# The recurrence of a two-layer trunk, issued in phases among the dense products: four steps a slot, its small TensorE products without priority

## The chip, the cores and the metric

One NeuronCore of a Trainium2 chip runs the whole program in one launch. The metric is the device time of one execution in microseconds (us). The engines are PE (TensorE, matrix products; PEld is its weight load), DVE (VectorE), ACT (ScalarE), POOL (GpSimd) and SP (which issues the DMAs). Each engine works through its own queue in order, and a semaphore holds an instruction back until what it reads is there.

## The reference, cut to what matters

The model has two layers. Each is SwiGLU, mixer, SwiGLU, with residual adds and a norm ahead of each. The mixer of layer 0 is RWKV-7, that of layer 1 is mLSTM. 512 prompt rows and 32 sample rows (8 sequences of 4) go through it, 544 columns in all.

```python
def rwkv7_time_mix(xn, shift0, S0, ...):
    xr, xw, xk, xv, xa, xg = [xf + xx * mu[c] for c in range(6)]
    r, k, v = xr @ wr, xk @ wk, xv @ wv
    w = -softplus(-(w0 + tanh(xw @ w1) @ w2)) - 0.5
    a = sigmoid(a0 + (xa @ a1) @ a2);  g = sigmoid(xg @ g1) @ g2
    def step(S, inp):
        sa = einsum('bhvk,bhk->bhv', S, -kk_t)
        S = S * d_t + sa[..., None] * b_t + v_t[..., None] * k_t
        return S, einsum('bhvk,bhk->bhv', S, r_t)
    y = groupnorm(scan(step, S0, ...)) + bonus
    return (y * g) @ wo
```

## The kernel before, in words

**Dense products.** Activations lie transposed, 128 features by columns. Columns are cut into two parts: part 0 has 256, part 1 has 288 (256 prompt columns and the 32 of the sample). A weight block comes by DMA into `wr`; ACT casts it to a high half `wh`, DVE subtracts to get the low half `wl` (lines 352 and 353), 512 columns at a time, four buffers of each. `mm3` (lines 355 to 358) then makes three fp32r products of each 128 by 128 block into a PSUM bank `pd`, of which there are two.

**The recurrence.** It works on head pairs. A group `m` is two pairs in one part: groups 0 to 3 are part 0, groups 4 to 7 are part 1. For each group `rwkv_prep` makes decays and keys (tiles `swa`, `a`), `rwkv_quad` squares up a 64 by 64 triangular inverse for its chunks (tiles `b`, `ti`, `p1s`, `tf`), `rwkv_tokens` lays out the values (`uv`), and then four chunks of 64 columns follow each other in `rwkv_chunk`: products into `pr`, `pu`, `pn` (one bank, `pc`), with DVE and ACT copies between, and a new state `sm`. `rwkv_finish` (norm, gate; lines 1151 to 1169) closes a group, `rwkv_sample` does the 32 sample rows of part 1. All their products are small: 64 to 128 rows, 64 to 128 columns mostly, in f32 or f16.

**Slots.** One chunk is a slot, `t` from 0 to 31; slots 0 to 15 are part 0. `rwkv_slots` writes the recurrence of a slot first and then some units of dense work: the rest of the first SwiGLU of part 1 and the first projections of part 1 in slots 0 to 9, its other projections in 10 to 15, nothing in 16, and the output projection of part 0 (`rwkv_out`) with the second SwiGLU of part 0 in 17 to 31. Before the projections of part 1 stands its norm (a product `pd<-rms`), and ahead of each kind of projection a mix: eight times `m` (line 693), a cast, and `mx` (line 695, on DVE and POOL in turn).

**What sets the order.** A list scheduler places every instruction on its engine as soon as it counts it as ready, by priority, and the priority is the place in the program. Inside `high_priority(OFF)`, with OFF = 20000, it counts as 20000 places earlier. The whole recurrence stands inside such a block, so that each of its instructions goes ahead of the dense work as soon as the scheduler has it ready.

Of the kernel before, what the change touches and what calls it, by code (L numbers as in the profile page):

```python
# [17 lines left out]
P = 128  # L18
D = 1024
KT = 8  # L20
# [8 lines left out]
OFF = 20000  # L29
NMX = 19  # L30
# [218 lines left out]

class Trunk:  # L250
    def __init__(self, tc, nc, a, o, pool):
        self.tc, self.nc, self.a, self.o, self.pool = tc, nc, a, o, pool
        self.n = 0
        self.last = None
        self.hn = {}
        self.V, self.S, self.G, self.T = nc.vector, nc.scalar, nc.gpsimd, nc.tensor

# [97 lines left out]
    def mm3(self, out, wh, wl, xh, xl, start, stop):  # L355
        self.T.matmul(out, wh, xh, start=start, stop=False)  # L356
        self.T.matmul(out, wh, xl, start=False, stop=False)  # L357
        self.T.matmul(out, wl, xh, start=False, stop=stop)  # L358
# [102 lines left out]
    def ffn_units(self, name, g, i, groups=(0, 8, 15, FT)):  # L461
# [18 lines left out]
        def up(m):  # L480
            pg, pu = self.bank("pd", 2), self.bank("pd", 2)
            for ps, n in ((pg, "_g"), (pu, "_u")):
                wt = self.weight(self.a[name + n][m])
                for k in range(KT):
                    c = slice(k * P, (k + 1) * P)
                    self.mm3(ps[:, :w_], *wt(c), xs[k][0], xs[k][1], k == 0, k == KT - 1)
            s, w, e = self.t1(w_), self.t1(w_), self.t1(w_)
            V.tensor_tensor(s, pg[:, :w_], rs, op=ALU.mult)  # L488
            V.tensor_tensor(w, pu[:, :w_], rs, op=ALU.mult)
            self.sigmoid(e, s)  # L490
            G.tensor_tensor(s, s, w, op=ALU.mult)
            G.tensor_tensor(s, s, e, op=ALU.mult)
            h[m] = [self.hm(w_) for _ in range(2)]
            self.split(*h[m], s)
# [9 lines left out]
        for k0, k1 in zip(groups, groups[1:]):  # L504
            us += [lambda m=m: up(m) for m in range(k0, k1)]
            us += [lambda m=m, k0=k0, k1=k1: down(m, k0, k1) for m in range(KT)]
# [50 lines left out]
    def rwkv(self, before=None, after=None):  # L557


        with self.scope("rw", nps=1):  # L560
# [4 lines left out]
            with self.tc.tile_pool(name="spill", bufs=1, space=DRAM) as dp:  # L565
# [3 lines left out]
                self.d, self.quad, self.st = {}, {}, {}  # L569
                self.chain, self.chain_y = [self.bank("pc", 2) for _ in range(2)]  # L570
                self.nhm = {"mx": NMX, "hm": 8}
                with self.scope("rw1", nps=0):
# [7 lines left out]
                    with self.tc.high_priority(OFF):  # L580
                        self.rwkv_ahead(0)
                        self.rwkv_square(0)
# [3 lines left out]
                    with self.tc.high_priority(OFF):  # L586
                        self.rwkv_value(0)
                        self.rwkv_ahead(1)
# [6 lines left out]
                with self.scope("rw2", nps=0):  # L595
                    with self.tc.high_priority(OFF):
                        self.rwkv_value(ND)
# [106 lines left out]
    def rwkv_project(self, n, c, i):  # L704
# [12 lines left out]
        return [lambda: xs.extend(self.rwkv_mix(c, i))] + [lambda m=m: unit(m) for m in range(KT)]  # L717

    def rwkv_low_rank(self, i):
# [36 lines left out]
        for c, ns in ((1, (("r_w1", P, slice(0, 64), self.hwa),)), (4, (("r_a1", P, slice(64, P), self.hwa),)),  # L756
                      (5, (("r_g1a", P, slice(0, P), self.hg), ("r_g1b", P, slice(0, 96), None)))):
            us.append(lambda c=c: mix(c))
# [3 lines left out]
    def rwkv_first(self, i):  # L762

        low, k = self.rwkv_low_rank(i), self.rwkv_project("k", 2, i)
        return ([lambda: self.rwkv_norm(i)] + low[:4] + self.rwkv_project("r", 0, i) + k[:5],
# [26 lines left out]
    def rwkv_ahead(self, m):  # L792

        if m < 2 * ND:
            self.d[m] = [self.rwkv_prep(2 * (m % ND) + a, m // ND) for a in range(2)]

    def rwkv_square(self, m):
        if m < 2 * ND:
            self.quad[m] = self.rwkv_quad(self.d[m])

    def rwkv_value(self, m):
        if m < 2 * ND:
            uv = self.rp("uv", 2, [P, 1024]).rearrange("p (a c h v) -> p a c h v", a=2, c=4, h=2)
            for a in range(2):
                self.rwkv_tokens(2 * (m % ND) + a, m // ND, self.d[m][a]["v"], uv[:, a])
            self.quad[m] += (uv,)

    def rwkv_slots(self, t0, t1):

        for t in range(t0, t1):  # L810
            m, c = divmod(t, 4)
            i, j = divmod(m, ND)
            with self.tc.high_priority(OFF):
                if c == 0:
                    self.rwkv_square(m + 1)

                    if m + 1 != ND:
                        self.rwkv_value(m + 1)
                if c == 2:
                    self.rwkv_ahead(m + 2)  # L820
                if i and c in (0, 1):
                    self.rwkv_sample(2 * j + c, self.d[m][c])
# [27 lines left out]
    def rwkv_prep(self, j, i):  # L850
        nc, V, S, G, T = self.nc, self.V, self.S, self.G, self.T
# [10 lines left out]
        for e, rows in enumerate(R):  # L862
            ps = self.bank("pq", 1)[:, :w]
# [12 lines left out]
        S.activation(q, k, AF.Square, scale=self.vec("kk", j))  # L876
        ps = self.bank("pq", 1)[:, :w]
# [29 lines left out]
        return {"xc": xc, "xs": xs, "arc": arc, "ars": ars, "pc": pc, "y": k, "v": v}  # L907

    def rwkv_quad(self, ds):
# [3 lines left out]
        V, S, G, T = self.V, self.S, self.G, self.T  # L913
# [16 lines left out]
        xt = self.rp("xt", 2, [P, 1024])  # L930
        mask = self.maskg.unsqueeze(1).to_broadcast([P, 4, P])
        for a, d in enumerate(ds):
            xc, arc = d["xc"], d["arc"]
            pg = pb()
# [6 lines left out]

        for a, d in enumerate(ds):
            px = self.bank("pq", 1)
            for i in range(4):
                T.transpose(px[:, i * P:(i + 1) * P], flat(d["xc"][:, i]), self.ident)
            S.copy(xt[:, a * 512:(a + 1) * 512], px)
# [10 lines left out]
        e = part(0)  # L957
        pt = pb()
# [5 lines left out]
        for l in range(1, 6):  # L964
            e = part(l)
            p1 = pb()
            each(lambda r, a, b: T.matmul(p1[r, a], e[r, a], ti[r, a], start=True, stop=True))
            p1s = h16("p1s")
            S.copy(p1s, p1[:, :W])
            pd = pb()  # L970
# [7 lines left out]
        pt = pb()  # L978
        each(lambda r, a, b: T.matmul(pt[r, a], ti[r, a], id16[r], start=True, stop=True))
        S.copy(tt, pt[:, :W])  # L980
        pr = pb()

# [615 lines left out]
```

## Time and profile before

| | us |
|---|---|
| median of 3 runs (lowest, highest) | 2540.12 (2539.03, 2542.99) |
| the profiled execution | 2541.78 |
| its span, first to last instruction | 2539.80 |
| PE busy, weight loads busy | 2445.1, 2310.1 |
| DVE, ACT, POOL busy | 1587.1, 1250.3, 501.6 |
| mean granted TensorE clock | 0.976 |

The chunks of the recurrence run from 423 us to 1100 us of the span, its last products at 1212 us. Before and behind it are dense products alone, and the mLSTM stage from about 1840 us. A matmul's row has a duration that is longer than the pitch at which such products follow each other, since they are pipelined; for the cost of a product the distance from start to start is read. The granted clock has two levels, 2.4 GHz (1.00) and 1.2 GHz.

### The profile page before, as it was taken

The numbers are of one execution on the slowest core, as the hardware profiler recorded it, in microseconds if no ns is written. First come the engines' busy times: TensorE is split into PE (matmuls) and PEld (weight loads), VectorE is DVE, ScalarE is ACT, GpSimd is POOL, SyncE is SP. The second block draws the span as 40 slices with busy tenths as digits, with TensorE's granted clock in tenths as the row PEclk, the third lists the DMA queues.
The fourth block names the chain that finished last, engine by engine and source line by source line (L and its number), as shares of the span: only waits on it lengthen the run. The fifth ranks groups of instructions, "written<-read, shape, count | busy, mean of one in ns | idle before, by whom it ended". The sixth has DMA issues, their size and how long they took to land.

```text
span 2539.8 us, 54086 instructions
## 1 busy us (share of the span) xinstructions
PE 2445.1 (96%) x21731; PEld 2310.1 (91%) x21731; DVE 1587.1 (62%) x3154; ACT 1250.3 (49%) x2716; POOL 501.6 (20%) x522
## 2 busy tenths in 40 slices
PE   9998999999889999999999999999999999999997
PEld 8998988888778788897899999999978899999997
DVE  6667787787887886765666544443346856444433
ACT  6555666655575564554555433332245545333322
POOL 1203333333432342322011011110000000111100
PEclk9998999999799899999999999999999999999999
DMA  6664543333233223444455522222223322222222
GB/s 215 183 197 130 166 131 120 105 96 120 90 120 103 75 93 113 129 150 146 128 167 164 153 89 90 84 85 88 83 87 112 101 73 92 86 92 90 88 84 73
DMA packets 102218, 291.62 MB, mean 115 GB/s; under 512 B 12568, under 2 KB 28344, under 8 KB 101968
## 3 DMA queue, kind: packets, MB, share of 16 engines
q1 hardware_dynamic: 101968, 288.18, 36.9%
q8 instruction: 170, 2.79, 0.4%
q14 instruction: 80, 0.66, 0.1%
HBM read 278.76 MB, written 9.38 MB: 113 GB/s over the span
## 4 chain that ended last, share of the span: by engine, by line
PE 84%; DVE 9%; issue 2%; ACT 2%; DMA 1%; POOL 1%; SPq 0%; DVEq 0%; ACTq 0%; POOLq 0%
PE ps L356 17%; PE ps L358 17%; PE ps L357 17%; PE pd L356 7%; PE pd L357 7%; PE pd L358 7%; DVE wl L353 2%; DVE m L693 1%; PE ps L1254 1%; PE ps L1256 1%; PE ps L1255 1%; PE b L937 1%; PE ps L1135 1%; DVE mx L695 1%; PE pc L1059 1%
## 5 line engine op out<-in xcount | busy, mean ns | idle before, releaser
L353 DVE TENSOR_TENSOR wl<-wr,wh 128x512 fp32r<-128x512 f32 (+2 forms) x1025 | 723.2, 708 | 479.6 <-ACT wh L352 452.8
L352 ACT CAST wh<-wr 128x512 fp32r<-128x512 f32 (+2 forms) x1025 | 621.8, 609 | 676.6 <-PE ps L357 430.8
L356 PE MATMUL ps<-a,wh 128*128 128x288 f32 (+1 forms) x2384 | 698.0, 293 | 13.5 <-ACT a L404 5.0
L358 PE MATMUL ps<-a,wl 128*128 128x288 f32 (+1 forms) x2384 | 692.6, 291 | 0.0
L357 PE MATMUL ps<-a,wh 128*128 128x288 f32 (+1 forms) x2384 | 686.6, 288 | 0.3
L356 PEld LDWEIGHTS ps<-a,wh 128*128 128x128 f32 x2384 | 452.8, 190 | 16.9 <-DVE raw L1350 5.4
L357 PEld LDWEIGHTS ps<-a,wh 128*128 128x128 f32 x2384 | 452.6, 190 | 1.5 <-DVE a L405 0.8
L358 PEld LDWEIGHTS ps<-a,wl 128*128 128x128 f32 x2384 | 450.0, 189 | 0.5 <-DVE wl L353 0.2
L428 POOL TENSOR_TENSOR t<-t,t 128x256 f32<-128x256 f32 (+1 forms) x132 | 141.7, 1073 | 846.7 <-ACT wh L352 410.1
L356 PE MATMUL ps<-h,wh 128*128 128x288 f32 (+1 forms) x1056 | 303.9, 288 | 0.0
L357 PE MATMUL ps<-h,wh 128*128 128x288 f32 (+1 forms) x1056 | 303.4, 287 | 0.0
L358 PE MATMUL ps<-h,wl 128*128 128x288 f32 (+1 forms) x1056 | 303.2, 287 | 0.0
L356 PE MATMUL pd<-rk,wh 128*128 128x288 f32 (+1 forms) x656 | 199.0, 304 | 6.8 <-DVE t L488 2.9
L358 PEld LDWEIGHTS ps<-h,wl 128*128 128x128 f32 x1056 | 198.9, 188 | 0.0
L357 PEld LDWEIGHTS ps<-h,wh 128*128 128x128 f32 x1056 | 198.9, 188 | 0.0
L357 PE MATMUL pd<-rk,wh 128*128 128x288 f32 (+1 forms) x656 | 198.6, 303 | 0.2 <-DVE gm L679 0.2
L356 PEld LDWEIGHTS ps<-h,wh 128*128 128x128 f32 x1056 | 198.6, 188 | 0.0
L358 PE MATMUL pd<-rk,wl 128*128 128x288 f32 (+1 forms) x656 | 197.2, 301 | 0.0
L352 ACT CAST h<-t 128x256 fp32r<-128x256 f32 (+1 forms) x132 | 55.3, 419 | 198.9 <-POOL t L428 198.9
L357 PE MATMUL pd<-mx,wh 128*128 128x256 f32 (+1 forms) x448 | 135.3, 303 | 9.4 <-DVE mx L695 6.6
L356 PE MATMUL pd<-mx,wh 128*128 128x256 f32 (+1 forms) x448 | 133.8, 302 | 4.3 <-ACT rk L716 1.9
L356 PEld LDWEIGHTS pd<-rk,wh 128*128 128x128 f32 x656 | 128.0, 195 | 10.5 <-ACT mx L694 2.9
(460 smaller groups left out, 4548.4 us busy)
## 6 DMA issues: line engine op xcount, KB each, us to landing
wr<-in_f0a_u_dram SPq DMA_DIRECT2D x44, 512.0 KB, 3.6
wr<-in_f0b_g_dram SPq DMA_DIRECT2D x44, 512.0 KB, 3.6
wr<-in_f0b_u_dram SPq DMA_DIRECT2D x44, 512.0 KB, 3.5
wr<-in_f0a_g_dram SPq DMA_DIRECT2D x43, 512.0 KB, 3.6
wr<-in_f0b_d_dram SPq DMA_DIRECT2D x24, 512.0 KB, 3.6
wr<-in_f1a_g_dram SPq DMA_DIRECT2D x22, 512.0 KB, 4.6
wr<-in_f1a_u_dram SPq DMA_DIRECT2D x22, 512.0 KB, 3.5
wr<-in_f1b_g_dram SPq DMA_DIRECT2D x22, 512.0 KB, 3.5
```

The lines of the kernel that those rows point to most:

```text
L352: self.S.copy(dst_h, src)
L353: self.V.tensor_tensor(dst_l, src, dst_h, op=ALU.subtract)
L356: self.T.matmul(out, wh, xh, start=start, stop=False)
L357: self.T.matmul(out, wh, xl, start=False, stop=False)
L358: self.T.matmul(out, wl, xh, start=False, stop=stop)
L428: self.G.tensor_tensor(s, s, w, op=ALU.mult)
L693: V.scalar_tensor_tensor(m, d, self.vec("mu", c * 8 + k), xn, op0=ALU.mult, op1=ALU.add)
L695: (self.G if k % 2 else V).tensor_tensor(l, m, h.bitcast(F32), op=ALU.subtract)
L937: T.matmul(pg[:, (1 - h) * 512 + i * P:(1 - h) * 512 + (i + 1) * P], flat(xc[R[h], i]), flat(arc[R[h], i]), start=True, stop=True)
L1059: T.matmul(py[R[h], out(a)], uv[:, a, c, h, :], gm[:, a, c, 1 - h, 64:128], start=True, stop=st is None)
L1135: T.matmul(pn[R[h], :], xt[H, h * 64:(h + 1) * 64], um, start=True, stop=True)
L1254: T.matmul(pss[q][:n, :], xs[k][0][:, ts], wt(cs)[0], start=k == 0, stop=False)
```

## The change

The functions of the recurrence become generators that yield before each group of products that waits for other engines, and name the PSUM bank it needs: "s" (none that is contended), "pq" or "ps". `rwkv_slots` starts the generators and, four times a slot, advances every one by a step at the "s" places, writes some dense work, advances those at "pq" and "ps", and writes dense work again. Dense work is now spread by its number of products (a SwiGLU unit in two halves, a mix counted as none). The products of the recurrence go through `Plain`, which takes the priority of 20000 back: they stand at their place in the program. The instructions of DVE, ACT and POOL keep it. The finish of a group is begun at the end of its last slot and advanced during the next, where it stood at once before.

```diff
+class Plain:
+    def matmul(self, *a, **k):
+        with self.t.tc.high_priority(LEAD - self.t.off):
+            return self.engine.matmul(*a, **k)
...
+    def rwkv_phase(self, places):
+        with self.tc.high_priority(OFF):
+            self.off = OFF
+            seen = set()
+            for name in list(self.gens):
+                place = self.gens[name][1]
+                if place in places and (place == "s" or place not in seen):
+                    seen.add(place)
+                    self.advance(name)
+            self.off = 0
...
     def rwkv_slots(self, t0, t1):
+        total, left, n = sum(c for c, _ in todo), 0, 2 * SPS * (t1 - t0)
+        def dense():
+            k += 1
+            while todo and done + todo[0][0] / 2 <= total * k / n:
+                c, f = todo.pop(0)
+                done += c
+                f()
         for t in range(t0, t1):
...
-                self.rwkv_chunk(m, c)
+                self.begin("chunk", self.rwkv_chunk(m, c))
+            for q in range(SPS):
+                self.rwkv_phase(("s",))
+                dense()
+                self.rwkv_phase(("pq", "ps"))
+                dense()
+                self.drain("chunk")
                 if c == 3:
-                    for a in range(2):
-                        self.rwkv_finish(2 * j + a, i, m)
-            self.step(-(-len(self.todo) // (t1 - t)))
+                    self.drain("finish", "sample")
+                    self.begin("finish", self.rwkv_finishes(m))
+                if t == 4 * ND or t == 8 * ND - 1:
+                    self.drain("finish")
```

SPS is 4, LEAD is 0. Smaller edits: the transposed rows `xt` are made apart from the quad; the quad's last transpose shares a bank with the residual; the sample's first products share banks, and two of its transposes one bank; in a chunk the products `py` stand ahead of the DVE instructions that make the new state.

Three places in the order of the built programs. The first is PE just around the norm of part 1. `uv_9791` is the values tile of group 3, `uv_7641` that of group 2. Before:

```order
L1042 MATMUL pc_2715<-sm_11215,tf_9789 64x64 x4
L387 MATMUL pd_8955<-rms_8932,c_c_all_79 128x288
L1059 MATMUL pc_2716<-gm_9376,uv_9791 64x64
L1048 MATMUL pc_2715<-uv_9791,xt_9377 64x64 x4
L1059 MATMUL pc_2716<-gm_9376,uv_9791 64x64 x3
L1035 MATMUL pc_2715<-uv_9791,gm_9376 64x64 x2
```

Now:

```order
L269 MATMUL pc_2715<-sm_9427,tf_9267 64x64 x4
L416 MATMUL pd_8878<-rms_8855,c_c_all_79 128x288
L269 MATMUL b_9476<-a_1622_8573 128x128 x8
L269 MATMUL ps_9706<-rk_930_4479,c_c_rw_2701 128x256
L269 MATMUL pq_9657<-c_c_all_79,x_69 64x64 x5
L269 MATMUL pc_2716<-gm_7640,uv_7641 64x64
```

The products `sm,tf` of 13 slots stand ahead of this norm in the order before, and of 9 now; at the last product of the projections of part 1 it is 16 in both.

The second is PE in that stretch of projections. `pd_9163` and `pd_8996` are banks of two dense units, `b_9716` is a step of the quad of group 3. Now:

```order
L385 MATMUL pd_9163<-mx_9115,wh_9166 128x288
L269 LDWEIGHTS ti_9572
L269 MATMUL b_9716<-p1s_9655,ti_9572 64x64
L269 LDWEIGHTS ti_9572
L269 MATMUL b_9716<-p1s_9655,ti_9572 64x64
L386 MATMUL pd_9163<-mx_9116,wh_9166 128x288
L387 MATMUL pd_9163<-mx_9115,wl_9167 128x288
L385 MATMUL pd_9163<-mx_9121,wh_9166 128x288
L269 LDWEIGHTS ti_9572
L269 MATMUL b_9716<-p1s_9655,ti_9572 64x64
```

The same step of an earlier group before, of which the 16 products follow each other:

```order
L358 MATMUL pd_6903<-rk_536_2749,wl_6945 128x288
L945 MATMUL pq_7840<-c_c_all_79,a_1392_7225 128x128 x4
L971 LDWEIGHTS ti_6235
L971 MATMUL b_6483<-p1s_6481,ti_6235 64x64
L971 LDWEIGHTS ti_6235
L971 MATMUL b_6483<-p1s_6481,ti_6235 64x64
```

The runs of small products that stand between dense ones are, up to the norm of part 1, to the end of its projections and to the end of the recurrence, 88, 36 and 126 before, and 96, 59 and 149 now.

The third is PE in slot 16. `stp` is the state that group 0 left, `pd_12858` and `pd_12895` are units of the output projection, `rk_2217_12033` is the finished output of the first pair of group 3. Before:

```order
L1118 MATMUL ps_12406<-sb_12404,sa_12363 64x64
L1061 MATMUL pc_2716<-a_1947_10340,stp_7438 64x64
L1059 MATMUL pc_2716<-gm_10796,uv_11877 64x64 x2
L1061 MATMUL pc_2716<-a_1957_10392,stp_7438 64x64 x2
L356 MATMUL pd_12858<-rk_1696_9082,wh_12861 128x256
L357 MATMUL pd_12858<-rk_1697_9083,wh_12861 128x256
L358 MATMUL pd_12858<-rk_1696_9082,wl_12862 128x256
```

Now:

```order
L269 MATMUL pc_2716<-a_1953_10283,stp_7499 64x64 x2
L269 MATMUL pq_12079<-rk_1812_9474,c_c_rw_2701 128x288
L269 MATMUL ps_12027<-a_519_2731,a_520_2732 128x256 x3
L269 MATMUL ps_12027<-a_520_2732 128x256
L269 MATMUL pc_2715<-uv_11822,gm_10743 64x64 x2
L269 MATMUL pc_2715<-sm_12024,a_1930_10119 64x64 x2
L269 MATMUL pc_2715<-uv_11822,gm_10743 64x64 x2
L269 MATMUL pc_2715<-sm_12024,a_1953_10283 64x64 x2
L269 MATMUL ps_12071<-sb_12010,sa_11909 64x64
L385 MATMUL pd_12159<-rk_2217_12033,wh_12166 128x256
L385 MATMUL pd_12225<-rk_2217_12033,wh_12232 128x256
L269 MATMUL pc_2715<-sm_12156,tf_11763 64x64 x4
```

Before, 18 dense products of one bank follow the chunk's; the finish of group 3 stands far ahead of them. Now the finish of group 3 (`ps_12027` is the gate of its first pair) stands in this slot, the first two units of the output projection hold both banks `pd` with all but their last products done, and from there to the last of these, after the finish of the second pair, 12 dense products stand among the small ones.

## Rows read from the trace of the kernel before

**Rows 1.** The page's first part: busy us, share of the span, instructions.
```profile
PE 2445.1 (96%) x21731; PEld 2310.1 (91%) x21731; DVE 1587.1 (62%) x3154; ACT 1250.3 (49%) x2716; POOL 501.6 (20%) x522
```
**Rows 2.** Busy time of each engine in stretches of the span; the first line names the columns.
```profile
core 0: us, PE busy (x) PEld busy (x) DVE busy (x) ACT busy (x) POOL busy (x), PEclk, DMA share, GB/s
420.00:640.00 220.00, 214.87 (x2758) 192.60 (x2756) 174.20 (x359) 134.07 (x312) 71.38 (x67) 0.99 0.36 109
640.00:806.00 166.00, 143.39 (x1221) 128.14 (x1222) 139.75 (x277) 105.87 (x263) 57.28 (x75) 0.87 0.30 93
806.00:1195.00 389.00, 379.02 (x4396) 329.41 (x4397) 275.72 (x585) 211.06 (x492) 126.49 (x129) 0.97 0.39 121
1215.00:1840.00 625.00, 624.29 (x4858) 623.44 (x4858) 319.75 (x579) 260.41 (x493) 71.12 (x66) 1.00 0.38 115
```
**Rows 3.** The same view, for line 357, one of three products of each dense block.
```profile
420.00:640.00 220.00, 99.44 (x331) 62.92 (x330) 0.99 0.36 109
```
**Rows 4.** PE in order of time, 1191 us: start, duration, engine, line, shapes.
```profile
1191.33 0.29 PE L357 MATMUL pd<-rk,wh 128*128 128x288 f32 x1
1191.46 0.29 PE L358 MATMUL pd<-rk,wl 128*128 128x288 f32 x1
1191.59 0.29 PE L356 MATMUL pd<-rk,wh 128*128 128x288 f32 x1
1191.72 0.29 PE L357 MATMUL pd<-rk,wh 128*128 128x288 f32 x1
1191.94 0.33 PE L1118 MATMUL ps<-sb,sa 64*64 64x64 f32 x2
1192.20 0.40 PE L358 MATMUL pd<-rk,wl 128*128 128x288 f32 x1
1192.43 0.29 PE L356 MATMUL pd<-rk,wh 128*128 128x288 f32 x1
```
**Rows 5.** DVE groups of 420 to 640 us: busy us, mean ns, idle before.
```profile
L353 DVE TENSOR_TENSOR wl<-wr,wh 128x512 fp32r<-128x512 f32 (+1 forms) x85 | 62.4, 738 | 17.7 <-ACT wh L352 15.7 <-ACT uv L1011 1.1
L502 DVE SCALAR_TENSOR_TENSOR x<-pd,x 128x288 f32<-128x288 f32 x32 | 14.3, 453 | 3.0 <-PE pd L358 2.8
L353 DVE TENSOR_TENSOR hm<-t,hm 128x288 fp32r<-128x288 f32 x11 | 5.9, 535 | 2.2 <-ACT hm L352 2.1
L489 DVE TENSOR_TENSOR t<-pd,rms 128x288 f32<-128x288 f32 x10 | 4.6, 457 | 4.2 <-PE pd L358 4.0
L488 DVE TENSOR_TENSOR t<-pd,rms 128x288 f32<-128x288 f32 x10 | 4.5, 455 | 2.3 <-PE pd L358 1.4 <-POOL t L491 0.7
L870 DVE TENSOR_TENSOR_SCAN swa<-c_c_scan,swa 128x256 f32<-128x256 f32 x5 | 3.7, 735 | 0.1
L1039 DVE COPY sm<-pc 128x128 f32<-128x128 f32 x12 | 3.4, 284 | 2.8 <-PE pc L1037 1.5 <-PE pc L1035 1.3
L374 DVE TENSOR_TENSOR rms<-rms,t 128x288 f32<-128x288 f32 x6 | 2.7, 452 | 0.0
```
**Rows 6.** The same of 640 to 806 us.
```profile
L693 DVE SCALAR_TENSOR_TENSOR m<-hm,c_vecs,x 128x288 f32<-128x288 f32 x48 | 31.1, 671 | 1.6 <-POOL mx L695 0.6 <-POOL hm L674 0.4
L695 DVE TENSOR_TENSOR mx<-m,mx 128x288 fp32r<-128x288 f32 x24 | 14.4, 601 | 0.8 <-ACT mx L694 0.5
L870 DVE TENSOR_TENSOR_SCAN swa<-c_c_scan,swa 128x288 f32<-128x288 f32 x4 | 3.6, 902 | 0.0
```
**Rows 7.** Busy time again, for the 60 us in which DVE is fullest.
```profile
720.00:780.00 60.00, 48.55 (x377) 42.96 (x376) 56.17 (x114) 40.53 (x97) 24.41 (x23) 0.89 0.28 88
```
**Rows 8.** PE in order of time at the last two finishes, 1200 to 1215 us.
```profile
1200.59 0.82 PE L1151 MATMUL ps<-rk,c_c_rw 128*128 128x288 f32 x2 [0.78 <-DVE s L1136]
...
1207.26 1.33 PE L1151 MATMUL ps<-rk,c_c_rw 128*128 128x288 f32 x2 [1.80 <-DVE rk L1169]
...
1214.72 0.81 PE L356 MATMUL pd<-rk,wh 128*128 128x288 f32 x2 [2.34 <-ACT rk L352]
```

More of the change, by code (lines that the diff above doesn't have):

```diff
@@ L480, in up, with half, second @@
         def up(m):
[L481 to L494, printed above, removed]
+            ps = []
+            def half(n):
+                ps.append(self.bank("pd", 2)[:, :w_])
+                self.part_dense(self.weight(self.a[name + n][m]), ps[-1], xs)
+            def second():
+                half("_u")
+                s, w, e = self.t1(w_), self.t1(w_), self.t1(w_)
+                V.tensor_tensor(s, ps[0], rs, op=ALU.mult)
+                V.tensor_tensor(w, ps[1], rs, op=ALU.mult)
+                self.sigmoid(e, s)
+                G.tensor_tensor(s, s, w, op=ALU.mult)
+                G.tensor_tensor(s, s, e, op=ALU.mult)
+                h[m] = [self.hm(w_) for _ in range(2)]
+                self.split(*h[m], s)
+            return Unit((24, lambda: half("_g")), (24, second))
         def down(m, k0, k1):
@@ L568, in rwkv @@
                 self.v = [[t[:, hs] for t in self.x] for hs in PARTS]
-                self.d, self.quad, self.st = {}, {}, {}
+                self.d, self.quad, self.st, self.xt, self.uv = [{} for _ in range(5)]
                 self.chain, self.chain_y = [self.bank("pc", 2) for _ in range(2)]
@@ L716, in unit @@
             self.S.copy(t, ps)
-        return [lambda: xs.extend(self.rwkv_mix(c, i))] + [lambda m=m: unit(m) for m in range(KT)]
+        return [Unit((0, lambda: xs.extend(self.rwkv_mix(c, i))))] + [lambda m=m: unit(m) for m in range(KT)]
     def rwkv_low_rank(self, i):
@@ L794, in rwkv_ahead @@
         if m < 2 * ND:
-            self.d[m] = [self.rwkv_prep(2 * (m % ND) + a, m // ND) for a in range(2)]
+            self.d[m] = []
+            for a in range(2):
+                yield from self.rwkv_prep(2 * (m % ND) + a, m // ND, self.d[m])
     def rwkv_square(self, m):
         if m < 2 * ND:
-            self.quad[m] = self.rwkv_quad(self.d[m])
+            yield from self.rwkv_quad(m, self.d[m])
     def rwkv_value(self, m):
@@ L993, in rwkv_quad, with rwkv_rows @@
         V.tensor_tensor(tf, tt, pf[:, :W], op=ALU.add)
-        return gm, tf, xt
+        self.quad[m] = gm, tf, self.xt[m]
+    def rwkv_rows(self, m):
+        self.xt[m] = xt = self.rp("xt", 2, [P, 1024])
+        for a, d in enumerate(self.d[m]):
+            yield "pq"
+            px = self.bank("pq", 1)
+            for i in range(4):
+                self.PT.transpose(px[:, i * P:(i + 1) * P], d["xc"][:, i].rearrange("p x t -> p (x t)"), self.ident)
+            self.S.copy(xt[:, a * 512:(a + 1) * 512], px)
     def wide_bank(self):
@@ L1061, in rwkv_chunk @@
                 T.matmul(py[R[h], out(a)], st[R[h], col(a)], arc[a][R[h], c, 1, :], start=False, stop=True)
+        sn = self.rp("stp", ND, [P, P]) if m < ND and c == 3 else self.rp("sm", 3, [P, P])
+        for a in range(2):
+            if st is None:
+                V.tensor_scalar(sn[:, col(a)], pn[:, col(a)], pc[a], None, op0=ALU.mult)
+            else:
+                V.scalar_tensor_tensor(sn[:, col(a)], pn[:, col(a)], pc[a], sp[:, col(a)], op0=ALU.mult, op1=ALU.add)
         if c == 3:
```

187 lines of the change are left out of this document (126 added, 61 removed).

## The prediction

> **What bounds the kernel now.** I read the page's first part, then the busy time by stretches, then the DVE groups of two stretches, then single products in order of time. The page says PE 96%, DVE 62% [rows 1], and the reader is to see that PE is the engine to look at, but that such a share is a mean over stretches with different limits. The stretches show it [rows 2]. Behind the recurrence (1215 to 1840 us) PE is busy 624.29 of 625 us at full clock: dense products alone, which the change does not touch. In the recurrence there are three kinds. From 420 us to the norm of part 1 (640 us) PE is busy 214.87 of 220: PE-bound, with DVE at 79%. From there to the end of the projections of part 1 (806 us) PE is busy only 143.39 of 166 at a granted clock of 0.87, and DVE 139.75, 84%: here the mixes load DVE (`m` and `mx` take 31.1 + 14.4 us of it [rows 6]) and PE waits for what DVE makes. From 806 to 1195 us PE is bound again (379.02 of 389), with DVE at 71%.
>
> Two prices are needed. **A slot.** In the first stretch the dense products are 331 for one of the three lines [rows 3]; at the pitch from start to start, 0.13 us [rows 4], 3 x 331 x 0.13 = 129 us. The other 91 us of the 220 are small products and what they wait for. The state copy `sm<-pc` stands there 12 times [rows 5], one a slot, so 7.6 us of PE a slot. Of DVE, 174.20 less the groups of dense work (62.4 + 14.3 + 5.9 + 4.6 + 4.5 + 2.7 = 94.4 [rows 5]) leaves 79.8, or 6.65 us a slot. **An interruption.** Two tiny products between dense ones [rows 4]: undisturbed the third start is 0.26 us after the first (1191.33 to 1191.59), with the interruption it is 0.71 us (1191.72 to 1192.43). That is 0.45 us, of which perhaps 0.1 is the products' own, an estimate from the 64-column shape beside 288 columns in 0.13; so 0.35 us for breaking the dense stream once, whatever stands in the break.
>
> **The change part by part.** It adds and removes almost no work: the order holds the same dense products and, but for some merged banks, the same small ones; I count those edits at nothing, since what they save is a few tiny products a group in a stretch with hundreds. What changes is where the small ones stand, and five terms follow.
>
> First stretch: the order has 13 slots ahead of the norm before and 9 now. It is PE-bound, so PE time leaves it: 4 x 7.6 = 30 us at most; by the count of small products that leave, about a quarter of what stood there, it is nearer 25. I take 28, range 21 to 31. The order has 8 more interruptions there, 8 x 0.35 = 3 us.
>
> Second stretch: the 4 slots arrive here, at 26.6 us of DVE and about 28 of PE. DVE then has 139.75 + 26.6 = 166 us of work, exactly the 166 it lasts now; PE, 143.39 + 28 + 23 more interruptions x 0.35 = 179 less what a full clock gives back (0.87 of 166 means 43 us at the half level; with PE busy half of them, half of that time is given back, 10 us), about 170. So both engines come to its present length with no idle time left, and neither can run without the other. If both overlapped wholly, the cost would be 0 to 4. At the share DVE has now (84%) it lasts 198, +32. At the fullest slice of DVE in the trace, 56.17 of 60 us [rows 7], 94%, it is 177, +11. I take 88%, 189 us, +23: nearer today's share, since that window holds no chunk chain to speak of.
>
> The Trainium skill, SBUF — State Buffer, section Who interferes with whom, says that a DVE instruction with two SBUF inputs contends with a GpSimd instruction that reads SBUF, and POOL makes half of the mixes' subtractions here. The trace agrees in kind: the scan takes 735 ns for 256 columns in the first stretch [rows 5] and 902 ns for 288 in the second [rows 6], 9% more than the columns explain. By that rule the 26.6 us of DVE would be 29 in the second stretch, and the sum 3 us higher.
>
> Third stretch: 23 more interruptions, 23 x 0.35 = +8 us (0.2 to 0.45 each: 5 to 10). Here PE is at 97%, so nothing covers them.
>
> The Trainium skill, TensorE: Matmul & The Clock Gate, section Step-by-step: what each phase is for, speaks against this price: the next product's weights are loaded while the present one runs, where row groups do not conflict or a background buffer takes them. Among dense products the trace agrees (a load of about 190 ns in a pitch of 130), at the change of kind [rows 4] it does not: 0.45 us for two tiny products. By the rule the interruptions would cost nothing, and the sum would be the one of the third rival.
>
> Slot 16: the finish of group 3 stood among dense products of the second stretch; now it stands in the slot that has no dense work of its own, and the first two units of the output projection wait for it with both banks `pd` held. PE has 12 dense products between. The chain of two finishes on nearly idle engines is read at the end of the recurrence: from 1200.59 over 1207.26 to 1214.72 us, 14.1 us [rows 8]. Small products of slot 16 fill it in part; a slot has 7.6 us of them and a sample step beside. What is left open is 14.1 - 7.6 = 6.5 us, and some slow clock behind it: +8, range 2 to 20. Behind this wait are the next units' dense products, which have no bank.
>
> The new order gives dependent small products more dense work between them in places, but the trace has little to win there: the idle time of PE is 10 us in 389 in the third stretch [rows 2]. I count that at nothing, and up to 5 us of gain in the first rival. DVE, ACT and POOL keep their priorities, so their instructions now stand ready earlier than PE delivers; what queues behind them on DVE are weight splits, with four buffers of lead. That cover gone, it is the DVE share of the second stretch, priced above. The tail is the same in both orders (last sample, two finishes, then dense), and in front of 420 us little moves.
>
> Sum: -28 + 3 + 23 + 8 + 8 = +14 us. It is made on the profiled execution (span 2539.80, time 2541.78, 1.7 us above the median of the runs); put on the median of 2540.1 it is **2554 us**.
>
> **The rivals.** *Balance wins* (the other side). The four slots that leave the PE-bound stretch find their place wholly in the idle time of the second, where PE has 23 us and DVE 26 us free, and since PE no longer starves, its clock stays up. It decides if DVE can run above 97% there. For it: the two idle times are about as large as what arrives. Against: they are the two halves of one chain, and the fullest 60 us have DVE at 94% [rows 7]. Price: -28 + 3 + 0 + 8 for the interruptions outside, no loss in slot 16, and 5 of the 10 us of slow clock: -22, 2518 us.
>
> *Starved twice* (slower). DVE keeps its 84% in the second stretch (+32), and the wait in slot 16 is open to its whole length with slow clock behind (+20), since the finish shares DVE and ACT with a chunk, a quad, a preparation and a sample: -28 + 3 + 32 + 8 + 20 = +35, 2575 us. For it: the dense banks are both held there; against: slot 16 has more small work than one slot's mean.
>
> *Interruptions are free.* Weight loads of the small products slip under the dense ones. For it: within the dense stream a load is hidden. Against: [rows 4]. Then -28 + 23 + 8 = +3, 2543 us, no change that can be told.
>
> **How the numbers follow.** The forecast gets 0.42, with a range of its own of 2543 to 2567; balance 0.30; starved twice 0.18; free interruptions 0.10. Two measurements of this kernel can tell about 0.2%, 5 us, from no change. Faster by more than that: 0.28 of the first rival and 0.02 of the third, 0.30. Within: 0.02 of the first, 0.08 of the third, 0.08 of the forecast's lower edge, 0.18. Slower: 0.34 and 0.18, 0.52. The range of 8 in 10 reaches from 2514, a little under the balance case, since the unknown share of DVE can fall on that side by as much, to 2584, past the starved case, whose slot 16 has no upper bound in a row.
>
> **What would show it.** Right: the time from the first chunk to the norm of part 1 is some 25 us shorter; from the norm to the last `mx` product it is 15 to 30 us longer with DVE near 90%; PE has a gap of several us with `ps` or `pd<-rk` products waiting for ACT or DVE between the last projection and the output projection's third unit; breaks of single small products among `pd` cost about 0.4 us. Wrong: the second stretch does not grow (balance), the third stretch becomes shorter by more than a few us, which would mean that waits which I read as PE's own work were given back, or a tail behind the last dense product of the recurrence that is longer than 14 us.

## The result and the profile after

| | before | changed |
|---|---|---|
| median, us (lowest, highest; 8 runs each) | 2539.57 (2537.9, 2543.13) | 2556.34 (2547.11, 2562.9) |
| ratio, 95% interval | 1 | 1.0063 (1.0046 to 1.008) |
| profiled execution, its span | 2541.78, 2539.80 | 2555.07, 2553.0 |

The change makes the kernel 0.63% slower, 16.8 us; 2554 us was predicted. The runs of the changed kernel lie further apart. The page's first part, which answers to [rows 1], shows 28 us more of PE and the same work elsewhere:

```profile
PE 2473.3 (97%) x21731; PEld 2321.6 (91%) x21731; DVE 1583.5 (62%) x3154; ACT 1253.9 (49%) x2716; POOL 497.4 (19%) x522
```

The stretches between the same four places of the program answer to [rows 2]: to the norm of part 1, to the last `mx` product, to the norm of the second SwiGLU, to the end of the recurrence (changed kernel; columns as there):

```profile
420.00:625.00 205.00, 199.25 (x2185) 175.75 (x2184) 154.84 (x314) 122.63 (x274) 57.23 (x57) 1.00 0.38 117
625.00:810.00 185.00, 170.37 (x1731) 146.17 (x1726) 157.49 (x308) 111.95 (x282) 68.58 (x83) 0.90 0.27 84
810.00:881.00 71.00, 66.84 (x910) 55.27 (x908) 49.33 (x109) 38.75 (x97) 15.53 (x16) 0.93 0.29 85
881.00:1210.00 329.00, 329.00 (x3531) 284.42 (x3529) 224.60 (x491) 179.51 (x412) 106.43 (x114) 0.99 0.41 124
```

These places are read from the start of their products, the first of a norm and the last of the other two:

| place, us | before | changed | longer by | predicted |
|---|---|---|---|---|
| norm of part 1 | 640.7 | 625.1 | -15.6 | -25 |
| last `mx` product | 806.9 | 809.9 | +18.6 | +23 |
| second norm | 865.5 | 880.6 | +12.1 | +8 |
| last finish | 1207.9 | 1222.9 | -0.1 | +8 |
| end of the span | 2539.8 | 2553.0 | -1.8 | 0 |

The total came out as forecast, and each line has the right sign or is nearly nothing. The lines add to 13.2 us, the difference of the two profiled executions; the medians lie 16.8 apart. In the second stretch DVE is at 85% and PE at 92%, about as assumed. The third and fourth line (to the second norm, to the last finish) are best read together, since work moved across their border: 713 records of small products stand between the last `mx` product and the second norm, where 503 did, and behind it 1929 where 2099 did. Together they are 12.0 us longer; +16 was predicted. The same two stretches before:

```profile
807.00:866.00 59.00, 55.33 (x700) 45.89 (x699) 49.81 (x106) 33.28 (x79) 16.82 (x15) 0.91 0.32 104
866.00:1195.00 329.00, 322.70 (x3692) 282.52 (x3691) 225.91 (x480) 176.88 (x413) 109.67 (x115) 0.98 0.40 123
```

In the last of them PE now never stops; before, it waited there by name for single results (waits of PE in the kernel before, 866 to 1195 us: engine, line waited for, us in total, times, longest):

```profile
PE ps L1118 <- DVE sb L1121: 2.2, 1, 2.2
PE pc L1048 <- ACT uv L1045: 1.4, 1, 1.4
PE ps L1104 <- ACT sa L1099: 1.2, 1, 1.2
PE b L967 <- DVE ti L976: 1.2, 1, 1.2
```

The same view of 881 to 1210 us in the changed kernel is empty. So some 6 us of waits are gone there; how the line's -0.1 divides between these, the added breaks and the work that moved out was not separated.

### The profile page after: what moved, and what is told of

Read it like the earlier page. It is cut to its first block, busy times and chain, and to the rows that moved or that the text cites. A ratio compares the mean times of both kernels' runs of the same rounds, so it can differ in the third digit from the quotient of the medians.

```text
span 2553.0 us, 54065 instructions
## 1 busy us (share of the span) xinstructions
PE 2473.3 (97%) x21731; PEld 2321.6 (91%) x21731; DVE 1583.5 (62%) x3154; ACT 1253.9 (49%) x2716; POOL 497.4 (19%) x522
## 4 chain that ended last, share of the span: by engine, by line
PE 87%; DVE 7%; ACT 2%; DMA 2%; issue 1%; POOL 1%; SPq 0%; DVEq 0%; ACTq 0%; POOLq 0%
PE ps L385 17%; PE ps L387 17%; PE ps L386 17%; PE pd L385 8%; PE pd L386 7%; PE pd L387 7%; PE pc L269 3%; PE b L269 2%; PE ps L269 2%; PE pq L269 1%; DVE wl L381 1%; DVE m L727 1%; PE ps L1387 1%; PE ps L1389 1%; PE ps L1388 1%
```

## The experiments

Theory T, the prediction's: the lost priority moves slots out of the PE-bound stretch into one with little room, and breaks the dense stream more often. Rivals: the phases cost; breaks are free; PE waits in slot 16.

**Each half alone.** Phases with the priority kept, which in `Plain` is one number:

```diff
-LEAD = 0
+LEAD = OFF
-        with self.t.tc.high_priority(LEAD - self.t.off):
+        with self.t.tc.high_priority(LEAD - self.t.off if self.t.off else 0):
```

> The changed kernel, but the small products keep their priority of 20000 (phases alone). In its order 13 slots stand ahead of the norm of part 1, as before, and the interruptions in the three stretches are 90, 35 and 113, against 96, 59 and 148. Theory (the lost priority moves slots into the second stretch and adds interruptions): the first stretch goes back to about 217 us, the second to about 168, and the whole to 2535 to 2545 us, that is 0.995 to 1.002 of the kernel before. Rival (the phases cost, by banks held over dense work and small products spread thin): the time stays near that of the changed kernel, 2550 to 2560 us, 1.004 to 1.008. Third: with fewer interruptions than before in the last stretch the phases alone gain 5 us or more.

Measured: 2541.76 us, ratio 1.0012 (1.0003 to 1.0021), within the theory's range; the norm of part 1 is at 644.6 us and the second stretch lasts 168.6. And the kernel before with `Plain` alone (`LEAD` 0), in `mm3` and, as here, in the six functions of the recurrence:

```diff
-        nc, V, S, G, T = self.nc, self.V, self.S, self.G, self.T
+        nc, V, S, G, T = self.nc, self.V, self.S, self.G, self.PT
```

> The kernel before, written as it was, but its small products lose their priority (the other half of the change alone). In its order 8 slots stand ahead of the norm of part 1 (13 before, 9 in the changed kernel), and the interruptions are 87, 58 and 158. Theory: first stretch 10 to 18 us shorter, second 18 to 25 us longer, the whole 10 to 20 us above the kernel before, 2550 to 2560, ratio 1.004 to 1.008. Rival (the phases are what costs): within 4 us of the kernel before. Third (the phases pay for themselves by giving waits back, and without them the written order waits more): above the changed kernel, 2560 to 2580, with idle time of PE in the last stretch above the 6 us of before.

Measured: 2541.57 us, ratio 1.0008 (0.9997 to 1.002): below the theory's range, as the first rival has it. In its profiled run (span 2545.0) the norm of part 1 is at 615.4, the last `mx` product at 802.5, the second norm at 867.5, the last finish at 1212.8: -25.3, +20.9, +6.4 and +2.9 us against before, where I had -25, +23, +8 and +8. So the stretch terms that I worked out come close to those of the priority alone, though five slots moved there and I had counted four; and that half costs 2.8 us in its median, which the interval does not tell from nothing. Both halves together cost 17: neither T nor the rival that the phases cost explains that by itself.

What the halves share was found by summing the distances from one start to the next over the products of the bank `pc`, from 380 us to the end of the recurrence: 88.0 us before, 92.0 with the priority alone, 109.0 with the phases alone, 108.3 in the changed kernel. Nearly half of the rise is one line: `uv,xt` (the 128-row products for the new state) takes 10.3 us before and 19.0 now. The trace shows how. PE in order of time, one chunk of the kernel before (f32 products stand in the records twice, so x8 is four):

```profile
944.85 0.45 PE L1048 MATMUL pc<-uv,xt 128*64 128x64 f32 x8
945.13 0.29 PE L1059 MATMUL pc<-gm,uv 128*64 128x64 f32 x4
945.35 0.33 PE L1061 MATMUL pc<-a,sm 64*64 64x64 f32 x4
945.61 0.34 PE L1059 MATMUL pc<-gm,uv 128*64 128x64 f32 x4
945.88 0.33 PE L1061 MATMUL pc<-a,sm 64*64 64x64 f32 x4
946.14 0.33 PE L945 MATMUL pq<-c_c_all,a 128*128 128x128 f32 x1
```

And a chunk of the changed kernel:

```profile
1005.00 0.34 PE L269 MATMUL pc<-uv,xt 128*64 128x64 f32 x4
1005.16 0.29 PE L269 MATMUL pc<-gm,uv 128*64 128x64 f32 x4
1005.28 0.28 PE L269 MATMUL pc<-uv,xt 128*64 128x64 f32 x2
1005.49 0.33 PE L269 MATMUL pc<-a,sm 64*64 64x64 f32 x2
1005.75 0.33 PE L269 MATMUL pc<-uv,xt 128*64 128x64 f32 x2
1006.00 0.33 PE L269 MATMUL pc<-a,sm 64*64 64x64 f32 x2
1006.26 0.34 PE L269 MATMUL pc<-gm,uv 128*64 128x64 f32 x4
1006.52 0.33 PE L269 MATMUL pc<-a,sm 64*64 64x64 f32 x4
1006.79 0.39 PE L385 MATMUL pd<-xs,wh 128*128 128x256 f32 x1
```

The same 24 records last 1.29 us from first start to next product before (944.85 to 946.14) and 1.79 now. The products `py` (`gm,uv` and `a,sm`) alternate with `uv,xt`, and each step between 128 rows (`128*64`) and 64 (`64*64`) takes about 0.15 us: over the trace 152 ns (36 times) from `uv,xt` to `a,sm` and 148 ns (29 times) back; from `uv,xt` to `uv,xt` before the mean is 33 ns (192 times). Inside this bank such a step occurs 85 times before, 132 times in the changed kernel and 139 times with the phases alone. The edit behind it is one that I had counted at nothing: `py` written ahead of the instructions that make the new state.

**That edit undone.** In `rwkv_chunk` of the changed kernel:

```diff
+        sn = self.rp("stp", ...)
+        for a in range(2):
+            ... # sn from pn, pc and sp
         out = lambda a: ...
         py = self.chain_y
         ... # products py
-        sn = self.rp("stp", ...)
-        for a in range(2):
-            ...
```

> The changed kernel with one small edit undone: in a chunk the products for the output (py) stand behind the instructions that make the new state again, as in the kernel before. Neither half of the change costs more than 3 us alone, both cost 17, so what I predicted from is not the whole. The traces show the small products of the chunks (bank pc) at 88 us before and 92 with the priority alone, but 109 and 108 in both kernels with phases; the products uv,xt go from 10 us to 19, since they now alternate with those of py: 128 rows in the order against 34. In this kernel's order they stand in 43 rows; its breaks of the dense stream are 310 against 303. Theory (alternation costs): pc falls to 95 to 101 us and the whole to 2544 to 2550, ratio 1.002 to 1.0045. Rival (the alternation only moves time between rows, the products wait for DVE and ACT anyway): pc stays within 4 us of 108 and the ratio within 0.001 of 1.0063.

Measured: 2544.12 us, ratio 1.0018 (1.001 to 1.0027), 12.2 us below the changed kernel; `pc` takes 96.1 us, 12.2 less. The theory holds, in the time and in the bank. Steps between 128 and 64 rows inside the bank are down from 132 to 84; 48 of them at 0.15 us in place of 0.03 are some 6 us, an estimate, so about half of the 12. The other half of the bank's fall was not traced to single steps. A chunk reads now as before (changed kernel with `py` behind, one dense product between):

```profile
993.72 0.45 PE L269 MATMUL pc<-uv,xt 128*64 128x64 f32 x8
994.61 0.39 PE L385 MATMUL pd<-xs,wh 128*128 128x256 f32 x1 [0.43 <-DVE x L534]
994.92 0.34 PE L269 MATMUL pc<-gm,uv 128*64 128x64 f32 x4
995.19 0.33 PE L269 MATMUL pc<-a,sm 64*64 64x64 f32 x4
```

The same edit on the phases alone:

> Phases with the priority kept, and py behind the state. Its order has 233 breaks of the dense stream, against 249 in the kernel before and 238 in the phases alone, and uv,xt in 33 rows. Theory (phases give breaks and waits back, and lose it to the alternation of py): 7 to 10 us below the phases alone, 2530 to 2535 us, ratio 0.997 to 0.9995, faster than the kernel before. Rival: no difference to the phases alone, ratio 1.000 to 1.002.

Measured: 2529.85 us, ratio 0.9972 (0.996 to 0.9984): faster than the kernel before, by 7 us, as the theory has it; `pc` at 97.3 us, with 84 such steps. And on the kernel before, the other way round:

> The kernel before with one edit: in a chunk the products py stand ahead of the instructions that make the new state. Its order has the same 13, 16 and 19 slots and the same 88, 36 and 125 breaks as the kernel before. Putting py behind the state took 12 us off the changed kernel and 12 off the phases alone, and the bank pc fell by as much in the traces. Theory (the alternation of uv,xt with py costs that, whatever else is changed): +8 to +14 us, 2547 to 2553, ratio 1.003 to 1.0055, with pc at 100 us or more. Rival (it costs only where the phases split the chunk): within 3 us of the kernel before, ratio 0.999 to 1.001, uv,xt near 10 us.

Measured: 2539.6 us, ratio 1.0006 (0.9996 to 1.0015), `uv,xt` at 10.1 us and `pc` at 88.3. The rival holds: there the scheduler puts PE's products in the same order however the lines stand, and the edit costs only where the phases split the chunk. Why the scheduler alternates them only there was not settled.

The ratios together:

| | priority kept | without priority |
|---|---|---|
| no phases, `py` behind | 1 | 1.0008 |
| no phases, `py` ahead | 1.0006 | not run |
| phases, `py` behind | 0.9972 | 1.0018 |
| phases, `py` ahead | 1.0012 | 1.0063 |

Within the phases `py` costs 0.0040 and 0.0045 (10 to 11 us), and the lost priority 0.0046 and 0.0051 (12 to 13 us). The dense stream is broken 225 times in the trace with priority and phases, 301 without the priority (`py` behind in both): 76 breaks and 14.3 us between the medians, 0.19 us a break. That is a quotient and not the price of a break, since slots moved as well.

**The price of a break by itself.** In the changed kernel, the first SwiGLU of layer 1, in each of its 88 groups of 24 dense products:

```diff
                         self.mm3(ps[:, :w_], *wt(c), ...)
+                        if name == "f1a" and k == 3:
+                            for q in (0, 64):
+                                self.T.matmul((pu if ps is pg else pg)[:64, 384 + q:448 + q],
+                                    wt(c)[0][:64, :64].bitcast(F32), xs[k][0][:64, q:q + 64].bitcast(F32), start=True, stop=True)
```

The second kernel leaves out `bitcast(F32)`; the third and fourth take all 128 rows, `[:, :64]`, without and with it.

> The changed kernel, with two more products of 64 by 64 by 64 in f32 in the middle of each of the 88 dense groups of the up projections of the first SwiGLU of layer 1, where nothing else than dense products runs; their result goes to unused columns and is never read. That stretch is at full clock with PE busy all the time, so its growth is the price of 88 interruptions and nothing else. Theory: 0.45 us each with the products' own time, so +31 to +40 us. Rival (the weight loads slip under the dense products and interruptions are free): 2 products of 0.03 to 0.1 us, so +5 to +15 us.

> The same 88 breaks with the same two products, but in fp32r like the dense ones around them. If it is the change of number type that breaks the stream (theory): +5 to +12 us, a quarter or less of the f32 breaks. If it is the change of shape, from 128 rows and 288 columns to 64 by 64: as much as the f32 breaks, +30 us or more. If interruptions are free: +5 us, the same as the f32 breaks within a factor of two.

> The 88 breaks again, two products in fp32r, but over 128 rows where the earlier ones had 64, and still 64 by 64 columns. With 64 rows a break took 0.32 us from the last dense start to the next, and one more pitch was 0.1 us longer behind it, in fp32r; 0.46 and 0.1 in f32. If it is the change from 128 rows to 64 and back that costs (theory now): 0.1 to 0.2 us a break, +9 to +18 us in all. If any change of tile shape or small column count costs: 0.3 to 0.4 us, +28 to +35.

> The same breaks over 128 rows in f32. If the rows cost (theory now): 0.15 to 0.3 us a break, the f32 products being twice as many, +13 to +26 us. If it is the number type: as the f32 breaks over 64 rows, 0.5 us and +44 us.

PE in order of time around a break (the `f32` in a row is the type of its output, which is the same for both), f32 and 64 rows:

```profile
1463.83 0.28 PE L387 MATMUL ps<-a,wl 128*128 128x256 f32 x1
1464.04 0.44 PE L453 MATMUL ps<-a,wh 64*64 64x64 f32 x4
1464.41 0.39 PE L385 MATMUL ps<-a,wh 128*128 128x256 f32 x1
1464.64 0.28 PE L386 MATMUL ps<-a,wh 128*128 128x256 f32 x1
```

fp32r, 64 rows:

```profile
1456.11 0.28 PE L387 MATMUL ps<-a,wl 128*128 128x256 f32 x1
1456.32 0.30 PE L453 MATMUL ps<-a,wh 64*64 64x64 f32 x2
1456.55 0.39 PE L385 MATMUL ps<-a,wh 128*128 128x256 f32 x1
1456.77 0.28 PE L386 MATMUL ps<-a,wh 128*128 128x256 f32 x1
```

fp32r, 128 rows:

```profile
1464.99 0.28 PE L387 MATMUL ps<-a,wl 128*128 128x256 f32 x1
1465.11 0.25 PE L453 MATMUL ps<-a,wh 128*64 128x64 f32 x2
1465.19 0.36 PE L385 MATMUL ps<-a,wh 128*128 128x256 f32 x1
1465.39 0.28 PE L386 MATMUL ps<-a,wh 128*128 128x256 f32 x1
```

f32, 128 rows:

```profile
1472.13 0.28 PE L387 MATMUL ps<-a,wl 128*128 128x256 f32 x1
1472.34 0.45 PE L453 MATMUL ps<-a,wh 128*64 128x64 f32 x4
1472.72 0.39 PE L385 MATMUL ps<-a,wh 128*128 128x256 f32 x1
1472.94 0.28 PE L386 MATMUL ps<-a,wh 128*128 128x256 f32 x1
```

A dense product follows the last after 0.12 us. Where type and rows stay (third), the small products follow as soon (1464.99 to 1465.11), and the next dense one 0.08 us after the first of them. In the other three the small ones begin 0.21 us after the dense one, the dense one comes some 0.15 us after the last small one, and the product behind that is 0.1 us late in all four. The weight loads show what changes. The first small load and the first dense one behind it, in the third kernel and then in the fourth:

```profile
1464.99 0.25 PEld L453 LDWEIGHTS ps<-a,wh 128*64 128x64 f32 x2
1465.17 0.19 PEld L385 LDWEIGHTS ps<-a,wh 128*128 128x128 f32 x1
```

```profile
1472.34 0.31 PEld L453 LDWEIGHTS ps<-a,wh 128*64 128x64 f32 x4
1472.72 0.19 PEld L385 LDWEIGHTS ps<-a,wh 128*128 128x128 f32 x1
```

In the third kernel the small load starts 0.12 us ahead of its product, as loads do in the dense stream, and the dense one 0.02 us ahead. In the fourth, and in the first two, both start together with their product, in all 88 breaks. From the last finish to the end of the span it is 1330.1 us in the changed kernel, and 1376.8, 1364.6, 1345.5 and 1379.1 here: by 88, 0.53 us a break, 0.39, 0.17 and 0.56, the two small products' own time included. The first comes out above its theory's range, the theory for the second falls (it is the change of shape), that for the third holds, that for the fourth falls: a change of type alone costs as much as a change of type and rows. Either change breaks the stream; free interruptions are out. These are one run each, and the stretch behind the last finish is read because the part ahead of it varies: with the same order of PE it ends at 1222.9 us in the changed kernel and at 1222.8, 1214.1, 1223.0 and 1230.2 here.

**Slot 16.** The finish of group 3 written out whole at the end of slot 15:

```diff
-                if t == 4 * ND or t == 8 * ND - 1:
+                if t == 4 * ND - 1 or t == 8 * ND - 1:
```

> The changed kernel, but the finish of group 3 is written out whole at the end of slot 15, so that the output projection finds it done. My prediction's term (the finish holds both dense banks, PE waits): from the last mx product to the second norm the time falls from 71 to about 63 us, the whole by 5 to 8. Rival, which the trace of the changed kernel speaks for (PE is busy 67 of 71 us there, the stretch is longer because 210 more small products stand in it): the whole stays within 3 us of 2556, ratio 1.005 to 1.0075, and the work goes to the stretch in front.

Measured: 2549.84 us, ratio 1.0048 (1.0035 to 1.006). The profiled run has the span of the changed kernel, 2553.0; from the last `mx` product (811.6) to the second norm (877.7) it is 66.1 us, 4.6 less than there, and 2.5 us more in front of the norm of part 1. The interval overlaps with that of the changed kernel: inconclusive. The gain is 6.5 us by the medians, 3.8 by the ratios, and the intervals leave room for none and for 9. Nor do the 4.6 us of the stretch show it, since the changed kernel's own stretch varies as much: in the first two kernels of breaks, which have the same order there, it lasts 74.5 and 66.7 us, at granted clocks of 0.84 and 0.99:

```profile
807.00:882.00 75.00, 71.52 (x908) 59.21 (x908) 49.90 (x110) 39.09 (x99) 16.08 (x16) 0.84 0.28 84
807.00:873.00 66.00, 62.06 (x897) 51.50 (x897) 48.48 (x107) 38.42 (x97) 14.91 (x15) 0.99 0.31 90
```

**DVE in the second stretch.** All low halves of the mixes on POOL:

```diff
-            (self.G if k % 2 else V).tensor_tensor(l, m, h.bitcast(F32), op=ALU.subtract)
+            self.G.tensor_tensor(l, m, h.bitcast(F32), op=ALU.subtract)
```

> The changed kernel with the low halves of the mixes all on POOL, where DVE made every second one: 14 us of DVE leave the stretch of the projections of part 1, where DVE is busy 157 of 185 us. If DVE bounds that stretch (my prediction): norm to last mx 8 to 14 us shorter, the whole 2543 to 2550. If PE and its waits on single results bound it (PE is busy 170 of 185): within 4 us of 2556. If POOL becomes the bound there: 5 to 15 us longer.

Measured: 2568.31 us, ratio 1.0118 (1.0102 to 1.0134). The second stretch there:

```profile
632.00:823.00 191.00, 173.13 (x1728) 148.50 (x1727) 151.50 (x283) 112.33 (x281) 86.62 (x107) 0.87 0.27 82
```

DVE has 6 us less of work and the stretch is 6 us longer. The groups of `mx`, on POOL in this kernel, then on DVE in the changed one (busy us, mean ns, idle before):

```profile
L729 POOL TENSOR_TENSOR mx<-m,mx 128x288 fp32r<-128x288 f32 x48 | 45.1, 960 | 47.0 <-PE pd L387 31.9 <-ACT mx L728 13.3 <-ACT swa L821 0.7
```

```profile
L729 DVE TENSOR_TENSOR mx<-m,mx 128x288 fp32r<-128x288 f32 x24 | 15.3, 639 | 0.3 <-ACT mx L728 0.3
```

POOL is not full (86.62 of 191) but takes 960 ns where DVE takes 639, and the sum on DVE is not what the stretch lasts for in this kernel. Another 7.5 us lie ahead of the norm of part 1 (632.6 for 625.1); the edit moves the mixes of part 0 as well, and the order of PE differs. So the run does not say whether DVE bounds the stretch in the changed kernel. Whether shorter DVE work at the same delay would help was not tried.

**Where the slots belong.** Phases, `py` behind, and the small products 1000 places ahead:

```diff
-LEAD = OFF
+LEAD = 1000
```

> Phases and py behind the state, and the small products 1000 places ahead instead of 20000 (before) or 0 (the changed kernel). Its order has 16 slots ahead of the norm of part 1 (13 in the phases alone), all of part 0, and 237 breaks of the dense stream against 233. Theory (slots in the PE-bound first stretch cost PE what they cost elsewhere, and slots in the second stretch fill idle time): with none in the second stretch that one gets idle again, and the whole is 2530 to 2545, not faster than the phases with py behind (2530). Rival (the second stretch is bound by DVE, so that every slot out of it is a gain): 2515 to 2528.

Measured: 2538.75 us, ratio 1.0001 (0.9992 to 1.001). The theory holds. All 16 slots of part 0 stand in the first stretch. First that and the second stretch of this kernel, then those of the phases with full priority, which has 13 slots and 3:

```profile
420.00:653.00 233.00, 220.78 (x2851) 196.10 (x2851) 178.13 (x364) 135.50 (x317) 66.64 (x64) 0.98 0.34 101
653.00:823.00 170.00, 138.17 (x1165) 123.33 (x1165) 135.13 (x255) 99.08 (x243) 56.63 (x75) 0.83 0.30 94
```

```profile
420.00:638.00 218.00, 209.29 (x2735) 189.04 (x2734) 174.11 (x359) 133.27 (x311) 69.15 (x65) 0.99 0.38 111
638.00:805.00 167.00, 141.43 (x1216) 126.08 (x1216) 135.84 (x264) 100.91 (x250) 56.45 (x75) 0.85 0.30 91
```

Three slots more make the first stretch 16 us longer (norm at 653.3 against 637.6) and their absence makes the second no shorter. So the first three slots are free in the second stretch. Four more, in the changed kernel with `py` behind, make it 7 us longer (174.1 for 167.0), and the first 17 us shorter.

Pair by pair, the traces tell where the lost priority costs. At the last `mx` product every kernel here has 16 slots done, and without the priority that product comes earlier each time: 802.5 for 806.9 us with no phases, 809.9 for 813.1 with phases and `py` ahead, 794.6 for 804.6 with `py` behind. With phases the loss lies behind the second norm: from there to the end of the span it is 1672.4 for 1647.6 us with `py` ahead and 1670.8 for 1640.8 with `py` behind. One slot more is left to do there in the first case and two in the second, and the dense stream is broken 130 times for 96 and 145 times for 94. What the breaks are of that was not tested, and these are one execution each.

## Why the prediction was right, and where not

The time was right, 2554 for 2556.34, by a sum in which errors cancelled: the first stretch gave 9.4 us less than predicted and slot 16 cost 4.1 more, the second and third stretch cost 4.4 and 8.1 less. That the total fits within 3 us is luck.

**The edits counted at nothing.** "I count those edits at nothing, since what they save is a few tiny products a group": this is the step that failed. It looked for products saved and not for the order in which those left follow each other. Moving `py` costs 11 to 12 us in the changed kernel, two thirds of its loss, as the kernel with that edit alone undone shows. It could have been seen: `uv,xt` stands in 34 rows of PE's order with the priority alone and in 128 in the changed kernel.

**The phases** were counted at nothing too ("up to 5 us of gain in the first rival"). Without `py` they gain 7 us where the priority is kept, and cost 2.5 where it is not, within the noise.

**First stretch,** -25 predicted, -15.6 measured; with the priority alone -25.3 with five slots gone. The lever is real, but a slot is worth less than the 6.2 us that -25 for four makes: 5.1 in the kernel with the priority alone, 5.1 with `py` behind (20.2 us for four), 5.2 at 1000 places (15.7 for three), breaks included. The other half of what is missing is `py` (the norm comes 4.6 us sooner with it behind). The row `sm<-pc` by which slots were counted is the copy of the chunk's right-hand side and not of the state; it stands once a slot too, so the count is right.

**Second stretch,** +23 and +18.6. Right in size, with DVE at 85% for the 88 assumed; that the share of DVE sets it is not shown. The 9% by which the scan seemed slower there is one instruction of four, 1346 ns beside work on POOL; the other three take 751 to 758 ns, no more than the columns explain. With `py` behind the stretch is 174.1 us long (620.5 to 794.6), +7.9. So 10.7 of the 18.6 us went when `py` went back; 82 small products of the order moved on to slot 16 with it, which grew by 5.2.

**Slot 16,** +8 and +12.1: right size, another cause in the main. PE is busy 66.84 of 71 us, its longest named wait is 1.8 us, and no gap of several us shows. What an earlier finish takes off is not told from the noise. What lengthens the stretch is more small products standing there: in the order 539, where before had 373.

**Third stretch,** +8 and -0.1. Part of this is work that moved into slot 16, 170 records of small products. The price of a break, 0.45 us in all, was not far off, but its row was misread: L1118 is one f32 product, which stands twice in the records, and not two; two of them measured alone cost 0.53. Also, summed over the starts that come more than 0.3 us later than such a product's usual distance, the waits of this stretch went from 19.5 to 14.4 us, those of the whole recurrence from 58.5 to 44.8: 14 us given back (11 to 19 by other choices of the usual distance), which I had refused to count ("little to win there").

**Theory T** holds in part. The move of slots is no loss: it brings the last `mx` product forward in all three pairs. What the lost priority costs within the phases, 12 to 13 us, lies behind the second norm, where the prediction had +8 for breaks.

**The rivals.** *Balance* and *Starved twice* did not occur: the second stretch grew, and not by 32. *Interruptions are free* is refuted for these products. The Trainium skill, TensorE: Matmul & The Clock Gate, section Step-by-step: what each phase is for, has the next product's weights loaded while the present one runs, where row groups do not conflict or a background buffer takes them; the third kernel of breaks agrees (its small loads start 0.12 us ahead), while in the three others the load starts with its product at each change of type or rows.

## What to carry to other kernels

Read the order of the small products as closely as their number: which shapes and types follow each other on TensorE is a cost of its own, and a scheduler may alternate two groups that the code writes apart. When a change has several edits, price the smallest too; here each half was near nothing alone and the sum was not. The version worth keeping is the phases with the priority kept and `py` behind the state: ratio 0.9972 (0.996 to 0.9984).

## What the runs showed of the hardware

A break of the stream of 128-row fp32r products by two small ones costs, with these, 0.17 us where they have the same type and rows, 0.39 with 64 rows, 0.53 and 0.56 in f32 with 64 and 128. At a change of rows or type the weight load starts together with its product; without one, 0.12 us ahead of it at the first small product. I had expected one of type and rows to matter; either does, and both together cost no more than the type alone. Among small f32 products a step between 128 and 64 rows takes 148 to 152 ns at each change.

The Trainium skill, TensorEngine Tiling (Array Packing), section Key Properties, says that a change of the tiling mode drains TensorE, while a change of tile within a mode does not. The steps between 128 and 64 rows agree, and so does the break in fp32r (0.39 us against 0.17). A change of the tile's columns alone, from 128 by 128 to 128 by 64, shows no such step (third kernel: 0.12 us, as within the dense stream). That a change from fp32r to f32 with the rows kept does the same is in these runs alone (0.56 us).
